# Delta net in a hybrid decoder layer: key norms and decay matrices among the convolutions, a PSUM bank of its own for the recurrence's key products, the output norm by chunks of tokens

## The chip, the cores and the metric

One core of one Trainium2 chip. The metric is the time that the device takes for one execution, in microseconds (us). Engines: TensorE (PE; PEld are its weight loads), VectorE (DVE), ScalarE (ACT), GpSimd (POOL), and SyncE (SP), which issues the DMAs. PSUM is the memory that PE's products are written to, in banks of 128 partitions by 512 float32 values; SBUF holds everything else.

## The reference

One step of one decoder layer for 1024 prompt tokens and 8 x 8 sample tokens, 1088 columns together, all in float32. Two feed-forward networks stand around a mixer; the mixer is what the change touches.

```python
x = x + 0.5 * rms_norm(swiglu_ffn(rms_norm(x, ...)), ...)       # D_MODEL 1024, D_FF 2816
qa, ka, va, qkvb, zb, ab, bb, ga, gb = split_columns(h @ w_in)  # h = rms_norm(x)
oa = swa_prompt(qa, ka, va, sinks)                              # window 128, 8 heads; swa_sample with a cache
xb = silu(causal conv of width 4 over qkvb)
qb, kb = l2_normalize(q) * 128 ** -0.5, l2_normalize(k)         # 4 heads, 128 wide
g = -exp(dn_a_log) * softplus(ab + dn_dt_bias);  beta = sigmoid(bb)
ob, s = gated_delta_chunked(qb, kb, vb, g, beta, s0)
ob = rms_norm(ob, dn_out_norm) * silu(zb)
merged = sigmoid(ga) * (oa @ w_branch_a) + sigmoid(gb) * (ob @ w_branch_b)
x = x + rms_norm(merged @ w_out);  x = x + 0.5 * (second feed-forward network)
...
# gated_delta_chunked, for each chunk of tokens: gc = cumsum(g)
decay = exp(gc_i - gc_j) for j <= i
m = strictly lower part of (beta k) @ k.T * decay;  solve (I + m) against [beta k exp(gc), beta v]
qk = (q @ k.T) * decay
def step(s, ...):
    v_new = v_u - k_cum @ s
    o = (q * exp(gc)) @ s + qk @ v_new
    s = s * g_tot + (k * exp(gc_last - gc)).T @ v_new
```

## The kernel before

**Columns and products.** Activations lie transposed: features on the partitions, the 1088 columns in three chunks (`CH`) of 384, 384 and 320. A float32 projection is made of three products of split values (high by high, high by low, low by high; lines 142 to 144). The three for one block of 128 features are called a *k-step* here; eight of them make one chunk of one *unit* of 128 output features. Projections write the banks `pa`. All other products of the mixer take banks from `pb()`, which gives `ph` and `py` in turn; `po` is one more bank, used by the attention's outputs (`po_tile()`, a single buffer).

**Order.** In the mixer PE's order is written out by hand. `queue` holds generators of projection units: `gate_unit` (ga), `z_unit` (z) and `conv_unit` (qkv: projection, convolution on DVE and ACT, SiLU; each head has one for k, q and v, in this order). `fill(us)` runs k-steps from the queue's head until their nominal times reach `us`; with an empty queue it does nothing. `finish` and `drain` run whole units. `together(a, b)` alternates between the two generators of a pair of heads: at each `yield x, y` it fills x after head a and y after head b. The other engines get their instructions in an order that a scheduler sets from the program.

**The mixer's stages**, with their approximate places in the profile: k, v, q projections to 848 us; decays of the tokens and transposes of the values (lines 773 to 810) to 854; `attention_prompt` over 16 items to 1003, whose output products, transposes and score products (L995, L979, L950) have fillers of 4.8 us between items; `attention_sample` to 1021; then for each pair of heads, 0 and 1, 2 and 3:
- their convolutions (those of head 0 serve as fillers in the attention),
- `first()`: key transposes (L1129) with copies and squares on ACT (L1130, L1131) and sums on DVE (L1132); decay matrices D and factors E from cumulated decays; the key norms, 9 columns wide (L149, L150, L1157 to L1169); q.k (L1175), D's transposes (L1177), their product on DVE (L1178), q times E on POOL (L1180); k.k (L1186) and M (L1189); value transposes (L1221),
- `invert()`: 62 DVE operations and some DMAs that invert 32x32 blocks, while PE runs `fill(51.0)`,
- `second()`: the blocks' inverse is completed; then the *recurrence*, eight steps of the state S for each head: M S (L1305) into columns 0 to 127 of a bank, U V of the next step (L1297), the key product (L1314, columns 128 to 255), the state's update on DVE (L1317), S q (L1323) and QK v (L1324) into columns 256 to 383, and a copy on ACT (L1325); then the *tail*: products with the eight sample states (L1336, 16 columns each), L1337, L1342, L1358, the sample states' update (L1366), and the output norm: sums over the head's features (L1374), the root and a Newton step over all 1088 columns, and the gate product on POOL (L1379).

After the second pair come the gate units 14 and 15 and the branch products (`br`), which need the heads' outputs, split in two (L196).

Of the kernel before, what the change touches and what calls it, by code (L numbers as in the profile page):

```python
# [7 lines left out]
F32 = mybir.dt.float32  # L8
# [27 lines left out]
def body(ctx: ExitStack, tc: tile.TileContext, d):  # L36
# [679 lines left out]

    hvd = cp.tile([P, 1], F32, tag="hvd", name="hvd")
    nc.vector.tensor_scalar_mul(hvd, vec[:, V_DN : V_DN + 1], -0.25)
    for cs in ((0, 1), (2,)):
        for u in (0, 2, 3, 4, 5, 1):  # L720
            w = wk if u == 0 and cs[0] == 0 else unit(U_K + u, f"kvq{u}_{cs[0]}")
            for c in cs:
                if u == 0:
                    do_ab(c)
                if u < 2:
                    mm = do_kv((kT, vT)[u], w, c)
                else:
                    mm = do_q(u - 2, w, c)
                if c == 1 and u in (0, 3):
                    tc.add_manual_dep(behind[u // 3].ins, mm.ins.name, NOSYNC, reason="behind products that are ready")  # L730
# [8 lines left out]
    tk = {}  # L739
    for nm, w in (("a", 36), ("x", 36), ("e", 36), ("u", 36), ("w", 36), ("z", 36), ("g", 36), ("beta", 36), ("bh", 36), ("gc", 36), ("gl", 36), ("kds", 36), ("bg", 36), ("gtot", 32), ("gts", 32), ("nea", 4)):  # L740
        tk[nm] = s2b.tile([P, w], F32, tag=f"tk_{nm}", name=f"tk_{nm}")
    def v94(t):
        return t.rearrange("p (c h) -> p c h", h=4)

    nc.vector.tensor_tensor(
        out=v94(tk["a"]), in0=atok[:, :, 0:4], in1=vec[:, V_DT : V_DT + 4].unsqueeze(1).to_broadcast([P, 9, 4]), op=ALU.add
    )
    nc.vector.tensor_scalar_mul(tk["x"], tk["a"], -1.0)
    nc.vector.tensor_tensor(out=tk["x"], in0=tk["x"], in1=tk["a"], op=ALU.min)
    nc.scalar.activation(tk["e"], tk["x"], AF.Exp)  # L750
    nc.scalar.activation(tk["nea"], vec[:, V_AL : V_AL + 4], AF.Exp)
    nc.vector.tensor_scalar_mul(tk["nea"], tk["nea"], -1.0)
    nc.vector.tensor_scalar_add(tk["u"], tk["e"], 1.0)
    nc.scalar.activation(tk["x"], tk["u"], AF.Ln)
    nc.vector.tensor_scalar_add(tk["u"], tk["u"], -1.0)
    nc.vector.tensor_scalar(out=tk["z"], in0=tk["u"], scalar1=0.0, scalar2=None, op0=ALU.is_equal)
    nc.vector.tensor_tensor(out=tk["u"], in0=tk["u"], in1=tk["z"], op=ALU.add)
    nc.vector.reciprocal(tk["w"], tk["u"])
    nc.vector.tensor_tensor(out=tk["x"], in0=tk["x"], in1=tk["w"], op=ALU.mult)
    nc.vector.tensor_tensor(out=tk["x"], in0=tk["x"], in1=tk["z"], op=ALU.add)  # L760
    nc.vector.tensor_tensor(out=tk["x"], in0=tk["x"], in1=tk["e"], op=ALU.mult)
    nc.vector.tensor_scalar_max(tk["a"], tk["a"], 0.0)
    nc.vector.tensor_tensor(out=tk["a"], in0=tk["a"], in1=tk["x"], op=ALU.add)
    nc.vector.tensor_tensor(
        out=v94(tk["g"]), in0=v94(tk["a"]), in1=tk["nea"].unsqueeze(1).to_broadcast([P, 9, 4]), op=ALU.mult
    )
    nc.vector.tensor_copy(v94(tk["beta"]), atok[:, :, 4:8])
    nc.scalar.activation(tk["beta"], tk["beta"], AF.Tanh, scale=0.5)
    nc.vector.tensor_scalar(out=tk["beta"], in0=tk["beta"], scalar1=0.5, scalar2=0.5, op0=ALU.mult, op1=ALU.add)
    nc.vector.tensor_scalar_mul(tk["bh"], tk["beta"], 0.5)  # L770
    psg = pb()
    g = tk["g"]
    nc.tensor.matmul(psg[:, 0:32], cst[:, C_TRI : C_TRI + P], g[:, 0:32], start=True, stop=True)
    nc.tensor.matmul(psg[:NSM, 32:36], cst[:NSM, C_TRIS : C_TRIS + NSM], g[:NSM, 32:36], start=True, stop=True)
    nc.tensor.matmul(psg[:, 64:96], ones, g[:, 0:32], start=True, stop=True)
    nc.tensor.matmul(psg[:NSM, 96:100], cst[:NSM, C_BONE : C_BONE + NSM], g[:NSM, 32:36], start=True, stop=True)
    for h in range(4):
        nc.tensor.matmul(
            psg[:, 128 + 8 * h : 136 + 8 * h], g[:NSM, 32 + h : 33 + h].to_broadcast([NSM, P]), cst[:NSM, C_BLK : C_BLK + 8], start=True, stop=True
        )  # L780
    for nm, o in (("gc", 0), ("gl", 64)):
        nc.vector.memset(tk[nm], 0.0)
        nc.vector.tensor_copy(tk[nm][:, 0:32], psg[:, o : o + 32])
        nc.vector.tensor_copy(tk[nm][:NSM, 32:36], psg[:NSM, o + 32 : o + 36])
    nc.scalar.activation(tk["gts"], psg[:, 128:160], AF.Exp)
    nc.vector.tensor_tensor(out=tk["kds"], in0=tk["gl"], in1=tk["gc"], op=ALU.subtract)
    nc.scalar.activation(tk["kds"], tk["kds"], AF.Exp)
    nc.scalar.activation(tk["gtot"], tk["gl"][:, 0:32], AF.Exp)
    nc.scalar.activation(tk["bg"], tk["gc"], AF.Exp)
    nc.vector.tensor_tensor(out=tk["bg"], in0=tk["bg"], in1=tk["beta"], op=ALU.mult)  # L790


    psc = pb()
    nc.tensor.transpose(psc[:36, :P], tk["gc"], ident)
    gct = s2b.tile([36, P], F32, tag="gct", name="gct")
    nc.vector.tensor_copy(gct, psc[:36, :P])
    for c in range(9):
        nc.sync.dma_start(gcd[:, c, :], gct[4 * c : 4 * c + 4, :])


    vtok = YA[6]
    vts = s2b.tile([NSM, P], F32, tag="vts", name="vts")
    for hlf in range(2):
        ps = py()
        for j in range(4):
            n = hlf * 4 + j
            nc.tensor.transpose(ps[:, j * P : (j + 1) * P], vT[:, n * P : (n + 1) * P], ident)
        nc.scalar.copy(vtok[:, hlf * 512 : hlf * 512 + 512], ps)
    ps = py()
    nc.tensor.transpose(ps[:NSM, :P], vT[:, NPR:NT], ident)  # L810
    nc.scalar.copy(vts, ps[:NSM, :P])
    for b in range(8):
        nc.sync.dma_start(d["vso"][b, 120:128, :], vts[b * 8 : b * 8 + 8, :])

# [122 lines left out]

    items = [(n, tp2) for n in range(8) for tp2 in range(2)]
# [159 lines left out]
    class Head:  # L1098
# [9 lines left out]
        def first(self):  # L1108
# [8 lines left out]
            nk = s2b.tile([P, 5, 9], F32, tag="nk", name=f"nk{h}", bufs=2)  # L1117
            ss, rho, rho2, t9, bgr = (nk[:, i, :] for i in range(5))
            nc.vector.memset(ss, 1.0)
# [4 lines left out]
            for c0 in (0, 4, 8):  # L1124
                n = 4 if c0 < 8 else 1
                w = P if c0 < 8 else NSM
                pt = pb()
                for i in range(n):
                    nc.tensor.transpose(pt[:w, i * P : i * P + P], kT_[:, (c0 + i) * P : (c0 + i) * P + w], ident)  # L1129
                nc.scalar.copy(wide(k, c0) if c0 < 8 else k8, pt[:w, : n * P])  # L1130
                nc.scalar.activation(M[:w, : n * P], pt[:w, : n * P], AF.Square)  # L1131
                nc.vector.tensor_reduce(  # L1132
                    out=ss[:w, c0 : c0 + n], in_=M[:w, : n * P].rearrange("p (i c) -> p i c", c=P), op=ALU.add, axis=AX.X
                )
# [18 lines left out]
            yield 2.0, 2.0  # L1153

            nc.scalar.activation(U, q, AF.Square, scale=P * EPS ** 0.5)
            nc.sync.dma_start(sqd[h], U)
# [12 lines left out]
            nc.vector.tensor_tensor(out=self.bhr, in0=mine("bh"), in1=rho, op=ALU.mult)  # L1169
            for j, c0 in enumerate((0, 4)):  # L1170
# [9 lines left out]
                nc.gpsimd.tensor_tensor(out=wide(q, c0), in0=wide(q, c0), in1=Es[j], op=ALU.mult)  # L1180
# [44 lines left out]
        def second(self):  # L1225
# [75 lines left out]
            for c in range(8):  # L1301
# [11 lines left out]
                yield 0.0, 0.8  # L1313
                nc.tensor.matmul(p[:, 128:256], k[:, cs], vns, start=True, stop=True)  # L1314
                S2 = ar[:, 4 + c % 2, :]
                if c > 0:
                    nc.vector.scalar_tensor_tensor(  # L1317
                        out=S2, in0=S, scalar=tk["gtot"][:, ix : ix + 1], in1=p[:, 128:256], op0=ALU.mult, op1=ALU.add
                    )
                else:  # L1320
                    nc.vector.tensor_copy(S2, p[:, 128:256])
# [5 lines left out]
                yield 0.0, 0.5  # L1327
# [12 lines left out]
            yield 0.0, 0.0  # L1340
# [21 lines left out]
            nc.scalar.activation(q, QK, AF.Square)  # L1362
            nc.vector.tensor_tensor(out=q, in0=q, in1=v, op=ALU.add)
# [8 lines left out]
            for a, b in ((0, 512), (512, 1024), (1024, NT)):  # L1372
# [269 lines left out]
```

## Time and profile before

| | us |
|---|---|
| median of 3 runs (2444.51 to 2445.79) | 2445.39 |
| the profiled execution | 2447.49 |
| its span, first instruction to last | 2445.6 |
| PE busy | 2368.5 (97%) |
| DVE busy | 1690.9 (69%) |
| ACT busy | 1091.3 (45%) |
| POOL busy | 44.2 (2%) |
| mean granted clock of PE | 0.986 |

The mixer stands between about 755 and 1490 us of the span; the feed-forward networks around it are not touched. In the rows of the profile L12 is line 12 of the kernel; a row of the waits says which engine, bank and line waited, for which engine and line, how long in all, how often, and the longest. A row of the timeline has the start, the duration, the engine, the line and the operation, the output and inputs with their shapes, and in brackets the idle time of that engine just before and what ended it. The granted clock is PE's, as a share of its full speed: at 0.5 a product takes twice as long.

### The profile page before, as it was taken

The numbers are of one execution on the slowest core, as the hardware profiler recorded it, in microseconds if no ns is written. First come the engines' busy times: TensorE is split into PE (matmuls) and PEld (weight loads), VectorE is DVE, ScalarE is ACT, GpSimd is POOL, SyncE is SP. The second block draws the span as 40 slices with busy tenths as digits, with TensorE's granted clock in tenths as the row PEclk, the third lists the DMA queues.
The fourth block names the chain that finished last, engine by engine and source line by source line (L and its number), as shares of the span: only waits on it lengthen the run. The fifth ranks groups of instructions, "written<-read, shape, count | busy, mean of one in ns | idle before, by whom it ended". The sixth has DMA issues, their size and how long they took to land. (4 is left out here: it accounts for less than half of the span.)

```text
span 2445.6 us, 38753 instructions
## 1 busy us (share of the span) xinstructions
PE 2368.5 (97%) x14535; PEld 2300.2 (94%) x14535; DVE 1690.9 (69%) x3385; ACT 1091.3 (45%) x2268; POOL 44.2 (2%) x33
## 2 busy tenths in 40 slices
PE   8999999999999999999899999999989999999997
PEld 7999999999998987999798979999989999999997
DVE  8887657757788567774497346556997576676677
ACT  7644424324475455543354333245744333233344
POOL 0000000000000000010101010000000000000000
PEclk9999999999999999999999989999999999999998
DMA  7332212213454511324222336435523122122453
GB/s 269 121 116 87 70 52 86 69 51 109 159 177 138 179 58 42 127 61 119 82 91 76 108 100 214 135 122 200 167 93 97 48 82 78 45 86 80 153 166 133
DMA packets 170373, 272.00 MB, mean 111 GB/s; under 512 B 34892, under 2 KB 74288, under 8 KB 170176
## 3 DMA queue, kind: packets, MB, share of 16 engines
q1 hardware_dynamic: 170184, 269.52, 34.2%
q8 instruction: 114, 1.87, 0.3%
q14 instruction: 75, 0.61, 0.1%
HBM read 227.03 MB, written 43.41 MB: 111 GB/s over the span
## 5 line engine op out<-in xcount | busy, mean ns | idle before, releaser
L467 PE MATMUL pa<-cl,h_c_s 128*128 128x384 f32 x704 | 236.5, 336 | 4.7 <-DVE cl L276 4.7
L466 PE MATMUL pa<-ch,h_c_s 128*128 128x384 f32 x704 | 237.6, 337 | 3.0 <-DVE t L472 2.7
L468 PE MATMUL pa<-ch,l_c_s 128*128 128x384 f32 x704 | 236.4, 336 | 0.0
L472 DVE TENSOR_TENSOR t<-pa,t 128x384 f32<-128x384 f32 x308 | 170.0, 554 | 83.1 <-PE pa L468 82.9
L466 PE MATMUL pa<-ch,h_c_a 128*128 128x384 f32 x528 | 177.1, 335 | 2.0 <-DVE t L472 1.5
L468 PE MATMUL pa<-ch,l_c_a 128*128 128x384 f32 x528 | 176.8, 335 | 0.0
L467 PE MATMUL pa<-cl,h_c_a 128*128 128x384 f32 x528 | 176.7, 335 | 0.0
L115 ACT CAST h_c_a<-r_c_a 128x512 fp32r<-128x512 f32 x132 | 81.8, 620 | 133.7 <-PE pa L467 113.5
L466 PEld LDWEIGHTS pa<-ch,h_c_s 128*128 128x128 f32 x704 | 132.9, 189 | 6.6 <-DVE t L472 6.2
L467 PEld LDWEIGHTS pa<-cl,h_c_s 128*128 128x128 f32 x704 | 133.0, 189 | 4.9 <-DVE cl L276 4.9
L468 PEld LDWEIGHTS pa<-ch,l_c_s 128*128 128x128 f32 x704 | 132.9, 189 | 0.0
L142 PE MATMUL pa<-xbh,h_ga 128*128 128x384 f32 (+1 forms) x384 | 130.7, 340 | 0.0
L115 ACT CAST h_c_s<-q_c_s 128x512 fp32r<-128x512 f32 x132 | 82.0, 621 | 104.1 <-PE pa L467 93.5
L143 PE MATMUL pa<-xbl,h_ga 128*128 128x384 f32 (+1 forms) x384 | 126.6, 330 | 0.0
L144 PE MATMUL pa<-xbh,l_ga 128*128 128x384 f32 (+1 forms) x384 | 126.6, 330 | 0.0
L466 PEld LDWEIGHTS pa<-ch,h_c_a 128*128 128x128 f32 x528 | 99.1, 188 | 2.8 <-DVE t L472 1.8
L468 PEld LDWEIGHTS pa<-ch,l_c_a 128*128 128x128 f32 x528 | 99.1, 188 | 0.0
L467 PEld LDWEIGHTS pa<-cl,h_c_a 128*128 128x128 f32 x528 | 99.1, 188 | 0.0
L142 PE MATMUL pa<-xbh,h_qkv 128*128 128x384 f32 (+1 forms) x288 | 95.6, 332 | 0.8 <-DVE t L884 0.8
L144 PE MATMUL pa<-xbh,l_qkv 128*128 128x384 f32 (+1 forms) x288 | 94.9, 330 | 0.0
L143 PE MATMUL pa<-xbl,h_qkv 128*128 128x384 f32 (+1 forms) x288 | 94.8, 329 | 0.0
L115 ACT CAST h_c_s<-r_c_s 128x512 fp32r<-128x512 f32 x44 | 27.4, 622 | 148.9 <-PE pa L467 134.7
(632 smaller groups left out, 7271.7 us busy)
## 6 DMA issues: line engine op xcount, KB each, us to landing
r_c_a<-in_up_dram SPq DMA_DIRECT2D x132, 256.0 KB
q_c_a<-in_up_dram SPq DMA_DIRECT2D x44, 256.0 KB
q_ub<-in_up_dram SPq DMA_DIRECT2D x44, 256.0 KB
r_ub<-in_up_dram SPq DMA_DIRECT2D x44, 256.0 KB
r_ua<-in_up_dram SPq DMA_DIRECT2D x42, 256.0 KB
q_ua<-in_up_dram SPq DMA_DIRECT2D x42, 256.0 KB
r_da<-in_dn_dram SPq DMA_DIRECT2D x40, 256.0 KB
q_da<-in_dn_dram SPq DMA_DIRECT2D x40, 256.0 KB
```

The lines of the kernel that those rows point to most:

```text
L115: nc.scalar.copy(hi, full)
L142: nc.tensor.matmul(ps[:, :n], hi[:, j, :], at(xh, k), start=first, stop=False)
L143: nc.tensor.matmul(ps[:, :n], hi[:, j, :], at(xl, k), start=False, stop=False)
L144: mm = nc.tensor.matmul(ps[:, :n], lo[:, j, :], at(xh, k), start=False, stop=last)
L466: nc.tensor.matmul(ps, wh[:, k, :], xh[:, k, :], start=k == 0, stop=False)
L467: nc.tensor.matmul(ps, wh[:, k, :], xl[:, k, :], start=False, stop=False)
L468: nc.tensor.matmul(ps, wl[:, k, :], xh[:, k, :], start=False, stop=k == 3)
L472: nc.vector.tensor_tensor(out=out, in0=ps, in1=other, op=ALU.add)
```

## The change

1. The tokens' decays become a function `decays()`, called among the q, k and v projections; the value transposes become `values()`, called after 4 k-steps of the first z unit.
2. `first()` is split into `decay()` (D and E), `keys()` (transposes and norms) and the rest. In pair 1, `a.keys()` and `b.keys()` follow head 1's convolutions of k and q; in pair 2 they follow those of q of the second head and v of the first. The value convolution of the second head is now directly ahead of q.k.
3. q times E goes from POOL (L1180) to DVE (L1230).
4. In the recurrence the key products of both heads go to the two halves of one `po` bank; the fillers of a step go from 0.8 + 0.5 to 0.4 us.
5. In the tail two places get fillers of 0.4 and 0.9; squares, norm and gate product go by the three chunks of columns, with the gate product on DVE (L1400) and a DMA for each chunk.
6. The attention's last item gets a filler of 8.5 us instead of 4.8, and ga4 joins the queue ahead of the sample's attention. Convolutions are run by `drain` and no longer through the queue.

```diff
+        fill(2.0)
+        values()
         attention_prompt()
-        queue += gates[3:4]
+        finish(list(queue))
+        queue += gates[3:5]
         attention_sample()
-        finish(list(queue))
-        queue += heads[1].conv
         for hs in (heads[0:2], heads[2:4]):
-            finish(list(queue))
-            queue += gates[4:10] if hs[0].h == 0 else zs[2:4] + gates[10:14]
-            together(*(x.first() for x in hs))
+            a, b = hs
+            if a.h == 0:
+                a.decay()
+                b.decay()
+                drain(b.conv[0])
+                a.keys()
+                drain(b.conv[1])
+                b.keys()
+                drain(b.conv[2])
+                queue += gates[5:10]
+            else:
+                for u in (a.conv[0], b.conv[0], a.conv[1]):
+                    drain(u)
+                a.decay()
+                b.decay()
+                drain(b.conv[1])
+                a.keys()
+                drain(a.conv[2])
+                b.keys()
+                drain(b.conv[2])
+                queue += zs[2:4] + gates[10:14]
+            together(a.first(), b.first())
             invert(hs)
...
-            fill(4.8 if 0 < it < n else 7.5)
+            fill(7.5 if it == 0 else 8.5 if it == n - 1 else 4.8)
...
-                nc.gpsimd.tensor_tensor(out=wide(q, c0), in0=wide(q, c0), in1=Es[j], op=ALU.mult)
...
+            for j, c0 in enumerate((0, 4)):
+                nc.vector.tensor_tensor(out=wide(q, c0), in0=wide(q, c0), in1=Es[j], op=ALU.mult)
...
-                yield 0.0, 0.8
-                nc.tensor.matmul(p[:, 128:256], k[:, cs], vns, start=True, stop=True)
+                yield 0.0, 0.4
+                pk = pks()[:, 128 * (h % 2) : 128 * (h % 2) + 128]
+                nc.tensor.matmul(pk, k[:, cs], vns, start=True, stop=True)
...
-                yield 0.0, 0.5
+                yield 0.0, 0.0
...
-            for a, b in ((0, 512), (512, 1024), (1024, NT)):
+            for a, b in CH:
+                cs = slice(a, b)
                 pq = pb()
-                nc.tensor.matmul(pq[:, : b - a], ones, q[:, a:b], start=True, stop=True)
-                nc.scalar.activation(k[:, a:b], pq[:, : b - a], AF.Identity, scale=1.0 / P, bias=eps4)
-            nc.scalar.activation(v, k, AF.Abs_reciprocal_sqrt)
-            newton(v, k, M)
-            nc.vector.scalar_tensor_tensor(out=QK, in0=QK, scalar=hvd, in1=v, op0=ALU.mult, op1=ALU.mult)
-            nc.gpsimd.tensor_tensor(out=QK, in0=QK, in1=U, op=ALU.mult)
-            nc.sync.dma_start(obd[h], QK)
+                nc.tensor.matmul(pq[:, : b - a], ones, q[:, cs], start=True, stop=True)
...
+                nc.vector.tensor_tensor(out=QK[:, cs], in0=QK[:, cs], in1=U[:, cs], op=ALU.mult)
+                nc.sync.dma_start(obd[h, :, cs], QK[:, cs])
```

PE's order in the recurrence of the first pair, from its first key product on. Before (`ph` and `py` are the two heads' banks; `pa` is a filler's):

```order
L1314 MATMUL ph_12336<-s_8355,s_8352 128x128
L1324 MATMUL ph_12336<-s_8354,s_8355 128x128
L1314 MATMUL py_12339<-s_8347,s_8340 128x128
L1324 MATMUL py_12339<-s_8346,s_8347 128x128
L142 MATMUL pa_12298<-xbh_1_8284,h_ga_1_12096 128x320
L143 MATMUL pa_12298<-xbl_1_8286,h_ga_1_12096 128x320
L144 MATMUL pa_12298<-xbh_1_8284,l_ga_1_12097 128x320
```

After, L1333 being the key product, L1343 the old L1324, L1323 the old L1305, and L1315 the old L1297:

```order
L1333 MATMUL po_12367<-s_8355,s_8352 128x128
L1343 MATMUL ph_12351<-s_8354,s_8355 128x128
L1333 MATMUL po_12367<-s_8347,s_8340 128x128
L1343 MATMUL py_12354<-s_8346,s_8347 128x128
L1323 MATMUL ph_12360<-s_8355,s_8351 128x128
L1323 MATMUL py_12362<-s_8347,s_8345 128x128
L1315 MATMUL ph_12382<-s_8350,s_8353 128x128
L1315 MATMUL py_12384<-s_8344,s_8341 128x128
```

Both heads' key products now write one `po` bank, and the step's end has no filler.

DVE's order at the end of the second head's value convolution in pair 1, after the change (L865 to L893 are the convolution, L1195 the product of q.k with D, L1230 that of q with E):

```order
L885 TENSOR_SCALAR t_963_11495<-t_962_11491,vec 128x64
L887 TENSOR_SCALAR t_964_11500<-t_962_11491,vec 128x64
L889 COPY sn_11503<-ncv 128x3
L890 COPY sn_11503<-t_962_11491 128x24
L888 TENSOR_TENSOR t_963_11495<-t_963_11495,t_964_11500 128x64
L1195 TENSOR_TENSOR s_8354<-ph_11520,s_8355 128x512
L887 TENSOR_SCALAR t_964_11500<-t_962_11491,vec 128x64
L1195 TENSOR_TENSOR s_8346<-ph_11534,s_8347 128x512
L888 TENSOR_TENSOR t_963_11495<-t_963_11495,t_964_11500 128x64
L1230 TENSOR_TENSOR s_8348<-s_8348,s_8355 128x512
```

Before, the sums and norms of the keys stood between the convolution and this product (L1178 then), with POOL doing q times E:

```order
L1132 TENSOR_REDUCE nk_11363<-s_8351 64x1
L1157 TENSOR_SCALAR nk_11363<-nk_11363 128x9
L1132 TENSOR_REDUCE nk_11432<-s_8345 64x1
L1178 TENSOR_TENSOR s_8354<-ph_11494,s_8355 128x512
L1157 TENSOR_SCALAR nk_11432<-nk_11432 128x9
L1178 TENSOR_TENSOR s_8346<-ph_11519,s_8347 128x512
L149 TENSOR_TENSOR nk_11363<-nk_11363 128x9
```

The norms are now ahead of this place, and the convolution's rest and the q-by-E products stand beside L1195.

More of the change, by code (lines that the diff above doesn't have):

```diff
@@ L728, in body @@
                     mm = do_q(u - 2, w, c)
+                if c == 2 and u == 4:
+                    decays()
                 if c == 1 and u in (0, 3):
@@ L757, in body @@
[L757 to L780, printed above, removed]
@@ L936, in gate_unit, with values @@
             yield from gate_do(i, w, c)
+    def values():
+        for hlf in range(2):
+            ps = py()
+            for j in range(4):
+                n = hlf * 4 + j
+                nc.tensor.transpose(ps[:, j * P : (j + 1) * P], vT[:, n * P : (n + 1) * P], ident)
+            nc.scalar.copy(vtok[:, hlf * 512 : hlf * 512 + 512], ps)
+        ps = py()
+        nc.tensor.transpose(ps[:NSM, :P], vT[:, NPR:NT], ident)
+        nc.scalar.copy(vts, ps[:NSM, :P])
+        for b in range(8):
+            nc.sync.dma_start(d["vso"][b, 120:128, :], vts[b * 8 : b * 8 + 8, :])
     items = [(n, tp2) for n in range(8) for tp2 in range(2)]
@@ L1106, in __init__, with decay @@
             self.conv = [conv_unit(u * 4 + h, A[u]) for u in (1, 0, 2)]
-        def first(self):
+        def decay(self):
             h = self.h
@@ L1122, in first @@
             DS, eR, DT = d8[:w8, 0, :], d8[:, 1, :], d8[:w8, 2, :]
[L1124 to L1134, printed above, removed]
             for j, c0 in enumerate((0, 4)):
@@ L1152, in first, with keys @@
             nc.scalar.activation(eR, QK[:, cs8], AF.Exp)
-            yield 2.0, 2.0
-            nc.scalar.activation(U, q, AF.Square, scale=P * EPS ** 0.5)
-            nc.sync.dma_start(sqd[h], U)
+            self.D = Ds, Es, DS, eR, DT
+        def keys(self):
+            h = self.h
+            q, kT_, v, M, k, U, QK, R = self.A
+            k8 = self.k8
+            nk = s2b.tile([P, 5, 9], F32, tag="nk", name=f"nk{h}", bufs=2)
+            ss, rho, rho2, t9, bgr = (nk[:, i, :] for i in range(5))
+            nc.vector.memset(ss, 1.0)
+            for c0 in (0, 4, 8):
+                n = 4 if c0 < 8 else 1
+                w = P if c0 < 8 else NSM
+                pt = pb()
+                for i in range(n):
+                    nc.tensor.transpose(pt[:w, i * P : i * P + P], kT_[:, (c0 + i) * P : (c0 + i) * P + w], ident)
+                nc.scalar.copy(wide(k, c0) if c0 < 8 else k8, pt[:w, : n * P])
+                nc.scalar.activation(M[:w, : n * P], pt[:w, : n * P], AF.Square)
+                nc.vector.tensor_reduce(
+                    out=ss[:w, c0 : c0 + n], in_=M[:w, : n * P].rearrange("p (i c) -> p i c", c=P), op=ALU.add, axis=AX.X
+                )
             nc.vector.tensor_scalar_add(ss, ss, 4.0 * EPS)
@@ L1223, in first, with second @@
             yield 0.0, 0.0
-        def second(self):
+        def second(self, pks):
             h = self.h
```

143 lines of the change are left out of this document (86 added, 57 removed).

## The prediction

> **What bounds the kernel now.** I read the page's totals and clock first, then the waits of TensorE (PE) between 750 and 1500 us, the mixer, the one stage whose code the change touches; then windows around them for the granted clock; then the timeline at the places that the change edits.
>
> ```profile
> span 2445.6 us, 38753 instructions
> PE 2368.5 (97%) x14535; PEld 2300.2 (94%) x14535; DVE 1690.9 (69%) x3385; ACT 1091.3 (45%) x2268; POOL 44.2 (2%) x33
> ```
>
> PE is the bound over the whole span: 2445.6 - 2368.5 = 77 us are idle. No matmul is removed, so the change can only take back idle time and time at half clock. The next two views say how much of either lies in the mixer: first the waits (PE bank, line <- what released it: us in total, times, longest), then windows (length, busy time of PE, PEld, DVE, ACT, POOL, granted clock, DMA).
>
> ```profile
> PE ph L1323 <- DVE s L1317: 6.5, 14, 0.6
> PE py L1323 <- DVE s L1317: 6.2, 14, 0.4
> PE ph L1186 <- DVE s L1178: 4.2, 2, 2.2
> PE ph L979 <- DVE s L833: 3.5, 1, 3.5
> PE pa L142 <- DVE t L1470: 2.5, 1, 2.5
> PE ph L1129 <- ACT s L1131: 2.3, 1, 2.3
> PE pa L142 <- DVE t L672: 2.1, 2, 1.4
> ```
> ```profile
> 850.00:858.00 8.00, 6.95 (x29) 6.02 (x29) 3.41 (x14) 3.50 (x15) 0.00 (x0) 0.57 0.14 41
> 977.00:981.00 4.00, 3.27 (x14) 3.30 (x15) 3.97 (x9) 1.77 (x5) 0.00 (x0) 0.57 0.06 12
> 1021.00:1025.00 4.00, 4.00 (x17) 3.96 (x16) 2.71 (x10) 2.51 (x5) 0.00 (x0) 0.57 0.39 108
> 1058.00:1073.00 15.00, 12.20 (x94) 11.68 (x92) 14.68 (x45) 9.80 (x24) 5.12 (x4) 1.00 0.15 50
> 1153.00:1194.00 41.00, 33.89 (x230) 30.77 (x231) 12.01 (x35) 11.79 (x39) 0.00 (x0) 1.00 0.18 58
> 1286.00:1304.00 18.00, 13.43 (x81) 12.63 (x79) 15.83 (x40) 11.07 (x27) 5.42 (x5) 0.81 0.20 66
> 1304.00:1309.00 5.00, 4.38 (x23) 4.03 (x24) 3.83 (x18) 1.17 (x2) 0.00 (x0) 0.66 0.01 2
> 1427.00:1449.00 22.00, 21.99 (x75) 14.15 (x74) 10.28 (x17) 6.47 (x13) 3.79 (x2) 0.61 0.43 132
> 1475.00:1490.00 15.00, 10.41 (x49) 9.48 (x48) 13.61 (x30) 10.43 (x24) 0.00 (x0) 0.89 0.94 293
> ```
>
> The seven waits add up to 27 us. A stretch at clock c for L us loses (1 - c) x L: 3.4, 1.7, 1.7, 3.4 (1286:1304), 1.7 (1304:1309), 8.6 and 1.7 us, 22 us in all. So some 50 us can be had in the stage; the sum below asks how much of it the edits reach.
>
> **E, the recurrence (two pairs of heads).** One step in the timeline of PE (start, duration), and the update of the state on VectorE (DVE):
>
> ```profile
> 1168.58 0.38 PE L1305 MATMUL ph<-s,s 128*128 128x128 f32 x2
> 1169.65 0.34 PE L143 MATMUL pa<-xbl,h_ga 128*128 128x384 f32 x1
> 1170.17 0.34 PE L143 MATMUL pa<-xbl,h_ga 128*128 128x384 f32 x1
> 1170.52 0.38 PE L1314 MATMUL ph<-s,s 128*128 128x128 f32 x2
> 1171.34 0.49 PE L1323 MATMUL ph<-s,s 128*128 128x128 f32 x2 [0.44 <-DVE s L1317]
> 1171.89 0.39 PE L1314 MATMUL py<-s,s 128*128 128x128 f32 x2
> 1172.72 0.49 PE L1323 MATMUL py<-s,s 128*128 128x128 f32 x2 [0.44 <-DVE s L1317]
> 1173.79 0.38 PE L1305 MATMUL ph<-s,s 128*128 128x128 f32 x2
> ```
> ```profile
> 1170.94 0.35 DVE L1317 SCALAR_TENSOR_TENSOR s<-s,tk_gtot,ph 128x128 f32<-128x128 f32 x1 [1.32 <-PE ph L1314]
> ```
>
> A step lasts 1173.79 - 1168.58 = 5.21 us: ten 128x128 products at 0.22 (1171.89 less 1171.34 is 0.55 for two, with a 0.1 restart), three filler k-steps at 0.52 (1170.17 - 1169.65), and twice 0.6 in which PE stands between L1314 and L1323 (0.82 apart instead of 0.22). The cause: L1314 and L1323 write the same bank, and DVE reads that bank in L1317, which starts 0.42 after L1314 and takes 0.35. After the change the key product goes to a bank of its own, so the query product of the same head no longer waits. But both heads share that bank: head b's product waits until head a's update has left it. By hand, from the start of head a's product: a's query product follows at 0.22, its last product at 0.44, and head b's key product could start at 0.66; the update is done at 0.42 + 0.35, and PE goes on 0.06 later, at 0.83. So it waits 0.17 once a step in place of 1.22. Head a's next use of the state comes far behind 0.83. The filler drops from three k-steps to one; the others are only run elsewhere. A step is then 10 x 0.22 + 0.52 + 0.17 = 2.9 us. Gain per pair 8 x 1.05 = 8.4, both 17. DVE and ScalarE (ACT) also evacuate filler, at half a microsecond each, and may stand ahead of an update: 12 is the lower bound; the whole of the stall, 8 x 1.22 x 2 = 19.5, the upper. I take 17, nearer to the top since the filler's share falls.
>
> **F, the tail behind each recurrence** (products with the sample states, norm sums).
>
> ```profile
> 1194.38 1.85 PE L1336 MATMUL ph<-mq,s 128*128 128x16 f32 x16
> 1212.46 0.42 PE L142 MATMUL pa<-xbh,h_qkv 128*128 128x384 f32 x1
> 1427.51 1.85 PE L1336 MATMUL ph<-mq,s 128*128 128x16 f32 x16
> 1449.18 1.02 PE L1374 MATMUL ph<-s,eye 128*128 128x512 f32 x2
> ```
>
> The first tail takes 18.1 us, the second about 23 (to the end of that row and a 64-column rest). The second lost 8.6 to the clock: the work is 14.4, so the excess is 8.6 + 3.7 = 12.3. In both the queue of fillers had run dry before the last waits. Since the recurrence will use 16 k-steps less per pair, the tail finds 1 + 2 + 4 + 10 of them, at the places where PE otherwise issues 16-column products that leave the clock low. I take -8.5; -4 if 16-column products halve the clock even with k-steps between; -11 if nearly all goes.
>
> **G, the branch products after the gates** wait 2.5 (L1470) and 2.1 (L672) and lose 1.7 to the clock: 6.3. They wait for splits of the heads' output on DVE, which come behind the last norm. Now the norm goes out in three chunks, with the gate product on DVE instead of the slower POOL, and 12 k-steps of ga13 (6.2 us) stand before these products. -4, from 0 (DVE is the limit here: 13.61 of 15 busy) to -6.3.
>
> **A, decays and value transposes** leave the empty place before the attention's first item and go among the k/v/q projections and behind 4 k-steps of z0. Window 850:858 shows PE idle for 1.05 and 3.4 lost: -3.5, from -2 to -4.5. **B, the attention's last items**: fill 8.5 instead of 4.8 at the last. The 3.5 wait (L979 for the softmax, with DVE busy 3.97 of 4 behind convolution work) comes before that fill, and moves only because the work before it shifts by some 4 k-steps; with the half clock behind it 5.2 are at stake. I take half, -2.5 (0 to -5.2). **C**, the half clock at 1021 (1.7): the sample's empty fill now finds ga4: -1 (0 to -1.7).
>
> **D, convolutions and first() of both pairs.** The old first(): PE, then DVE, then POOL.
>
> ```profile
> 1058.36 0.60 PE L1129 MATMUL ph<-eye,s 128*128 128x128 f32 x4
> 1065.46 1.05 PE L1175 MATMUL ph<-s,s 128*128 128x128 f32 x8
> 1070.34 0.60 PE L1177 MATMUL py<-eye,R 128*128 128x128 f32 x4
> 1073.15 1.16 PE L1186 MATMUL ph<-s 128*128 128x128 f32 x8 [2.21 <-DVE s L1178]
> ```
> ```profile
> 1058.56 0.42 DVE L672 SCALAR_TENSOR_TENSOR t<-pa,r 128x256 f32<-128x256 f32 x1
> 1063.31 0.22 DVE L897 TENSOR_TENSOR t<-t,t 128x64 f32<-128x64 f32 x1
> 1066.55 0.69 DVE L1178 TENSOR_TENSOR s<-ph,s 128x512 f32<-128x512 f32 x1
> 1069.26 1.34 DVE L150 SCALAR_TENSOR_TENSOR nk<-nk 128x9 f32<-128x9 f32 x2
> ```
> ```profile
> 1066.60 2.60 POOL L1180 TENSOR_TENSOR s<-s,s 128x512 f32<-128x512 f32 x2 [10.13 <-PE ph L1175]
> ```
>
> Now the key transposes, norms and decays stand among the convolutions, and q.k comes directly behind the value convolution. Removed: the two 9-column norm operations of 0.67 each while POOL's L1180 runs, and the 2.2 wait behind them. Added: q.k of head a's second half needs the bank that DVE frees in L1195 (old L1178), and in DVE's order L1195 stands behind the value convolution's rest: 1058.56 to 1063.31 is 4.8, less a reduction of 0.6, plus two 0.6 steps that moved in: L1195 ends about 6.2 us after the last convolution matmul. PE reaches that product after half of what q.k and the decay transposes take in all (1070.34 - 1065.46 + 0.43 = 5.3), 2.66: wait 3.6. The rest is DVE-paced: four L1195 and four of POOL's products, now on DVE, at 0.6 each, so that k.k starts 9.2 after the last convolution instead of 14.8 - 4.2 (fill) - 2.2 (transposes) = 8.4: +0.8. About +1 for the transposes' own waits among the convolutions, where ACT also changes tables. With a half clock behind the 3.6 (1.7): +3.5 in pair 1, whose old first() ran at clock 1.00. In pair 2 the old one had 4.6 idle, and 3.4 + 1.7 lost, so the same new state gives -2. Together +1.5; from -6 (DVE keeps up, no half clock) to +9 (DVE paces the convolutions too).
>
> Whether that half clock comes is the open point. In the rows, a wait of 2.2 within 1058:1073 left the clock at 1.00, while in pair 2 a wait of 2.0 ahead of 1304 was followed by 0.66.
> [...]
>
> **Sum:** E -17, F -8.5, G -4, A -3.5, B -2.5, C -1, D +1.5 = -35. The profiled span of 2445.6 becomes 2410.6. The profiled execution took 2447.5, 1.9 more, and the median of the runs is 2445.4, 2.1 below that: so 2410 for the median.
>
> **Rivals.**
> 1. *The shared bank becomes the new chain.* If filler evacuation on DVE stands ahead of the update in most steps, head b's product waits 0.9 (0.17 + 0.35 + 0.4) instead of 0.17: 16 x 0.73 = 12 back, 2422. For it: the bank serves both heads. Against: DVE is busy 12.01 of 41 in 1153:1194, and less filler runs than before.
> 2. *DVE paces convolutions and first().* D at +9: 2418. For it: DVE 15.83 of 18 and 14.68 of 15 in the old stages, and POOL's products added. Against: what blocked DVE behind POOL goes away.
> 3. *Nearly all idle goes*: A -4.5, B -5.2, C -1.7, D -6, E -19.5, F -11, G -6.3: 2391.
> 4. *Slower: the recurrence falls to half clock.* With one k-step instead of three it is nearly all 128x128 products; if these don't hold the clock, each step's 2.72 us doubles: 16 x 2.72 = +43, 2453. It decides from 13 of the 16 steps on (35 / 2.72). Against: 1153:1194 ran at 1.00 with 7.1 us of 41 idle, and 1065.46 to 1070.34, only such products, at 1.00 too.
>
> **Numbers.** The forecast (2402 to 2416) 0.50; rival 1 alone 0.12; rival 2 alone 0.16, both together 0.05 (2430); rival 3 0.11; rival 4 0.03; no change for a reason not seen 0.03. The range 2395 to 2428 leaves out the last two, the two rivals together, and most of rival 3. A difference of 0.2%, 5 us, is about what a measurement of this kernel tells from none: faster 0.94, same 0.03, slower 0.03.
>
> **What would show it.** After: the wait for the state's update at the query product gone, a wait of 0.2 to 0.3 at the second head's key product, a step of 2.9 us; clock near 1 in the second tail; a new wait of 3 to 5 us at q.k in each first(); the 2.5 at L1470 gone. The forecast is wrong if the recurrence step is over 3.5 us, or if the convolutions show waits for DVE in the projections' banks.

## The result, and the profile after

Median 2416.75 us (4 runs, 2412.53 to 2420.05) against 2444.95 (4 runs, 2438.46 to 2445.79): ratio 0.9889, 95% interval 0.9864 to 0.9915, so 28 us faster. Timed again beside the last experiment the same kernel gave 2416.79 and 0.989 (0.987 to 0.9911). The profiled execution took 2414.26 us and lies 2.5 us below the median of its runs, as that of before (2447.49) lies 2.5 above its own; its span, on which the accounts below are made, is 33 us shorter than that of before. 30 us of these lie in the mixer: from the same product ahead of it to the same product behind it, 761.7 us became 731.7. The other 3 lie in the second feed-forward network, which is not changed and whose length differs by as much from run to run (below).

The totals of the page after:

```profile
span 2412.4 us, 38783 instructions
PE 2354.2 (98%) x14535; PEld 2295.1 (95%) x14535; DVE 1688.5 (70%) x3437; ACT 1103.4 (46%) x2300; POOL 22.1 (1%) x21
```

PE's idle time went from 77 to 58 us, and its busy time fell by 14 with the same instructions. Some 8.5 us of the 14 are the clock: in the mixer 47.8 us ran at half clock before and 30.7 after, and half of such a stretch is lost (after, the 128x384 products at 971.5 to 972.1, at half clock, start 0.31 to 0.33 us apart, those from 972.9 on, at full clock, 0.17). The waits of PE in the mixer after:

```profile
PE ph L1192 <- DVE s L1195: 8.6, 2, 4.9
PE ph L983 <- DVE t L888: 3.1, 1, 3.1
PE ph L1255 <- DMA s<-ud: 2.1, 1, 2.1
PE pa L142 <- DVE t L1518: 1.0, 1, 1.0
PE po L1333 <- DVE s L1340: 0.5, 2, 0.3
```

The 12.7 us of waits in the recurrences are gone. The largest wait is now the one at q.k (L1192), which did not exist before. Windows after:

```profile
850.00:858.00 8.00, 7.76 (x51) 7.25 (x50) 3.55 (x9) 2.71 (x8) 0.00 (x0) 1.00 0.46 144
1020.00:1030.00 10.00, 10.00 (x76) 8.90 (x75) 2.98 (x12) 3.50 (x8) 0.00 (x0) 1.00 0.25 72
1062.00:1082.00 20.00, 15.80 (x109) 14.62 (x108) 17.96 (x53) 6.96 (x16) 0.95 (x1) 0.83 0.14 36
1156.00:1179.00 23.00, 22.66 (x171) 21.05 (x169) 11.49 (x34) 10.53 (x37) 0.00 (x0) 1.00 0.22 71
1274.00:1296.00 22.00, 16.46 (x118) 15.05 (x118) 19.27 (x64) 10.20 (x22) 2.33 (x1) 0.84 0.23 56
1393.00:1422.00 29.00, 28.50 (x130) 23.63 (x129) 11.96 (x26) 9.45 (x21) 3.79 (x2) 0.82 0.37 112
```

The decays' old place (850:858) and the sample's end (1020:1030) run at full clock (the latter not in every profile, see below); the recurrence (1156:1179) is almost without a gap; first() of either pair (1062:1082, 1274:1296) loses some 4 to 5.5 us idle and 3.5 to the clock; the second tail still loses 29 x 0.18 = 5.2 to the clock. One step of the recurrence after, on PE:

```profile
1163.85 0.39 PE L1323 MATMUL ph<-s,s 128*128 128x128 f32 x2
...
1165.31 0.38 PE L1333 MATMUL po<-s,s 128*128 128x128 f32 x2
1165.53 0.39 PE L1342 MATMUL ph<-s,s 128*128 128x128 f32 x2
1165.75 0.39 PE L1343 MATMUL ph<-s,s 128*128 128x128 f32 x2
1166.13 0.49 PE L1333 MATMUL po<-s,s 128*128 128x128 f32 x2
...
1166.90 0.39 PE L1323 MATMUL ph<-s,s 128*128 128x128 f32 x2
```

The query product (L1342) follows its key product at 0.22, as forecast, and head b's key product (1166.13) comes 0.38 after L1343 instead of 0.22: the forecast wait of 0.17 is 0.16. A step lasts 3.05 us, where the forecast had 2.9.

For each stage, its time less that of its products at the pace of undisturbed ones of the same shape, before and after in the two profiles:

| term | lost before | lost after | change | forecast |
|---|---|---|---|---|
| A projections and decays | 10.6 | 7.9 | -2.7 | -3.5 |
| B prompt attention | 37.5 | 37.8 | +0.3 | -2.5 |
| C sample attention | 3.7 | 1.7 | -2.0 | -1 |
| D convolutions and first(), pair 1 | 5.9 | 8.9 | +3.0 | +3.5 |
| D the same, pair 2 | 13.6 | 9.8 | -3.8 | -2 |
| inversion and start of second() | 2.8 | 5.0 | +2.2 | 0 |
| E recurrences | 23.5 | 6.1 | -17.4 | -17 |
| F tails | 13.0 | 8.6 | -4.4 | -8.5 |
| G branch products | 7.2 | 1.6 | -5.6 | -4 |
| sum | 117.8 | 87.4 | -30.4 | -35 |

### The profile page after: what moved, and what is told of

It is laid out like the page before. It is cut to its first block, busy times and chain, and to the rows that moved or that the text cites. A ratio compares the mean times of both kernels' runs of the same rounds, so it can differ in the third digit from the quotient of the medians.

```text
span 2412.4 us, 38783 instructions
## 1 busy us (share of the span) xinstructions
PE 2354.2 (98%) x14535; PEld 2295.1 (95%) x14535; DVE 1688.5 (70%) x3437; ACT 1103.4 (46%) x2300; POOL 22.1 (1%) x21
## 4 chain that ended last, share of the span: by engine, by line
PE 81%; DVE 9%; DMA 4%; ACT 3%; issue 2%; SPq 0%; DVEq 0%; ACTq 0%
PE pa L142 10%; PE pa L143 10%; PE pa L144 10%; PE pa L466 8%; PE pa L467 8%; PE pa L468 8%; PE py L349 3%; PE py L348 3%; PE ph L348 3%; PE ph L349 3%; PE ph L347 3%; PE py L347 3%; DVE t L865 1%; DMA q_da<-in_dn_dram 1%; DMA q_db<-in_dn_dram 1%
## 5 line engine op out<-in xcount | busy, mean ns | idle before, releaser
L144 PE MATMUL pa<-xbh,l_qkv 128*128 128x384 f32 (+1 forms) x288 | 94.1, 327 | 0.0
L143 PE MATMUL pa<-xbl,h_qkv 128*128 128x384 f32 (+1 forms) x288 | 94.1, 327 | 0.0
```

The source lines that it names most:

```text
L143: nc.tensor.matmul(ps[:, :n], hi[:, j, :], at(xl, k), start=False, stop=False)
L144: mm = nc.tensor.matmul(ps[:, :n], lo[:, j, :], at(xh, k), start=False, stop=last)
```

## Experiments

Each is the changed kernel with one edit; the last, best, joins three. Times are spans of one profiled execution beside 2412.4, and lengths of the mixer beside 731.7. Ten executions of the changed kernel had spans from 2410.6 to 2418.1, so a difference of a few us between two spans decides nothing; the mixer (731.6 in a second profile of the changed kernel), the waits and the lengths of the stages are read instead, and differences of under 1 us are not.

One thing blurs these too. In the mixer of the profiles before and after the granted clock is either full or half, and it was half for 3.41 us at a time (969.2 to 972.6 in the profile after), or for 6.83, 10.24 (after) and 17.07 (before), at 1.7 us lost for each 3.41. Where such a stretch falls moves with small shifts in time. At the sample's end, where the profiles of the changed kernel have none, the clock in 1018:1032 is 0.76 to 0.88 in e1, e3, e8, e9 and best, whose edits do not touch that place.

**Bank or fillers? e1.** The key product goes back into the step's own bank, with the fillers as changed.

```diff
-                pk = pks()[:, 128 * (h % 2) : 128 * (h % 2) + 128]
+                pk = p[:, 128:256]
```

> The changed kernel with the key product back in columns 128 to 255 of the step's own bank, fillers still 0.4. Theory 'bank' (the waits came from the query product writing the bank that the state's update reads): two waits of 0.6 us or more come back in each step, each recurrence grows by 8 to 12 us from 22.3, and the span goes from 2412 to 2428 to 2436. Rival 'fillers' (ACT and DVE were held up by the evacuation of the fillers, of which there are now a third): the recurrence stays within 3 us of 22.3, span 2412 to 2416.

Span 2437.7. The recurrences last 31.4 and 31.1 us instead of 22.6 and 22.2. Waits and one step on PE:

```profile
PE py L1342 <- DVE s L1336: 6.2, 14, 0.4
PE ph L1342 <- DVE s L1336: 6.1, 14, 0.4
```
```profile
1169.78 0.39 PE L1323 MATMUL ph<-s,s 128*128 128x128 f32 x2
...
1171.20 0.38 PE L1333 MATMUL ph<-s,s 128*128 128x128 f32 x2
1172.02 0.49 PE L1342 MATMUL ph<-s,s 128*128 128x128 f32 x2 [0.44 <-DVE s L1336]
...
1173.94 0.39 PE L1323 MATMUL ph<-s,s 128*128 128x128 f32 x2
```

The old 0.82 between key and query product is back, 28 waits of it, and the step is 4.16, 1.1 more. That is the forecast's 1.05. The span is 1.7 us over the bound given for the theory: the recurrences make 17.6 of the mixer's 21.5, the rest is in the tails (3.5) and small parts.

**e2** puts the fillers back (0.8 and 0.5 in place of 0.4 and 0).

> The changed kernel with the recurrence's fillers back at 0.8 and 0.5 us. Theory 'bank': a step is 2.9 plus two k-steps of 0.52, about 3.9 to 4.0, with no wait over 0.3 at the key or query products; the 32 k-steps are missing in the tails, so the span is 2414 to 2420. Rival 'fillers': waits of 0.4 to 0.6 come back at the query products, step 4.8 or more, span over 2424.

Span 2416.0; recurrences 31.1 and 30.2 us, that is 8.5 and 8.0 more for 16 k-steps of 0.52, with no wait at the query products:

```profile
PE pa L142 <- DVE t L1518: 3.1, 2, 2.0
PE po L1333 <- DVE s L1336: 1.0, 1, 1.0
PE po L1333 <- DVE s L1340: 0.7, 2, 0.5
```

So the bank alone ended the waits. Fewer fillers are a matter of where the k-steps go: the mixer is 5.5 longer. At its end the branch products (first row) wait 3.1 instead of 1.0. The larger loss is in the first tail, which now has no k-step instead of 17 and stands at half clock for 17.1 us (8.5 lost, beside 1.7 in the changed kernel):

```profile
1185.00:1208.00 23.00, 22.09 (x72) 13.76 (x73) 10.27 (x23) 7.50 (x17) 3.79 (x2) 0.63 0.39 119
```

**e3** issues both key products next to each other, by a `yield 0.0, 0.0` behind the key product.

> The changed kernel with both heads' key products issued next to each other, ahead of both updates. If head b's product waited for head a's update in each step (0.17 by the prediction's hand count, 16 times), the recurrences shrink from 22.6 and 22.2 us by 1 to 1.5 each, span 2409 to 2411. If the count was wrong and nothing waits there in most steps, they stay within 0.4 and the span within 1 us of 2412.

Span 2409.2; recurrences 20.9 and 20.3, 1.7 and 2.0 shorter, and the wait of L1333 is gone from the list. The prediction's wait at the shared bank was there in every step: 0.16 in all steps but three, longer (0.5 and 0.3) in the first step of each pair and shorter (0.1) in one last step. That makes 1.6 and 1.4 us; what the other 0.1 and 0.6 are was not traced.

**Was it worth it to spread the key norms? e7** puts all convolutions first, then both `keys()`.

> The changed kernel with all convolutions first, then both heads' key transposes and norms, then the rest of first(). Theory 'DVE order' (q.k's bank is freed late because the value convolution's rest stands ahead on DVE): the key part moves the same wait to the key transposes and norms, so from the last convolution to the first k.k it takes about 14 us instead of 11.9 in pair 1 and 14 in place of 12.5 in pair 2, in sum 2 to 6 us more, span 2414 to 2420. Rival (putting the norms among the convolutions brought nothing, DVE's total decides): span within 2 us of 2412.

Span 2412.1, mixer 730.0: no loss, as the rival had it. From q.k to k.k it takes 8.0 and 7.5 us instead of 11.9 and 12.5, and what the key transposes wait cancels it: from the sample attention or the first tail to the end of the value transposes it takes 58.0 and 94.1 us, beside 58.2 and 93.9. The waits:

```profile
PE ph L1192 <- ACT s L1159: 3.1, 2, 1.6
PE ph L1157 <- ACT s L1159: 2.7, 2, 1.8
PE py L1157 <- ACT s L1159: 1.9, 2, 0.9
```

7.7 in sum in place of 8.6 at L1192, and the wait for the inversion's DMA is not in this profile. The part of the change that its name puts first brought nothing measurable. What PE waits for differs, though: DVE with the rest of the value convolution in the changed kernel, ACT with the copies and squares of the key transposes (L1158, L1159) here. So it is not DVE's total that decides, as the rival's wording says, but two engines in turn at about the same price.

**e5** fills that wait: `fill(4.8)` ahead of `together(a.first(), b.first())`.

> The changed kernel with a 4.8 us filler (10 k-steps) between the last convolution and first() in both pairs. Theory 'DVE order': PE only waited for DVE to finish the value convolution's rest; the waits of 3.8 and 4.9 at q.k fall below 1 in sum, the half clock behind them (6.8 in the profile, four windows) goes, span 2398 to 2404. Rival 'DVE total': the fillers' own evacuations delay DVE as much, waits of 5 us or more remain, or the time comes back where the 20 k-steps now lack (tails, branch products): span 2408 to 2413.

Span 2408.0, mixer 724.8: 7 us shorter. The same stretches, from the filler to k.k:

```profile
1061.00:1077.00 16.00, 16.00 (x129) 15.45 (x128) 15.51 (x46) 6.94 (x14) 0.00 (x0) 1.00 0.23 66
1268.00:1287.00 19.00, 19.00 (x147) 18.49 (x146) 18.72 (x62) 10.70 (x21) 0.00 (x0) 1.00 0.21 63
```

PE is busy all of the time, at full clock; DVE nearly so. The 8.6 us of waits and 6.8 of lost clock (6.83 us at half clock in each pair) are gone, and q.k to k.k takes 5.4 and 5.3. Of these 15.4 us more than half came back: the branch products wait 3.2 in sum instead of 1.0 and then stand at half clock for 3.41 us, and the first tail, with 8 k-steps instead of 17, loses 5 us to the clock instead of 1.7. The span is the rival's lower bound; the mechanism is the theory's, the return the rival's second half.

**e8** takes the output norm whole again, with the gate product on POOL.

> The changed kernel with squares, norm and gate product over all 1088 columns again, the gate product on POOL. Theory 'chunks' (the branch products no longer wait since the last norm goes out by chunks): waits of 3 to 5 us come back ahead of the branch products, span 2415 to 2420. Rival 'cover' (12 k-steps of ga13 in front of the branch products did it): these waits stay within 1.5 us, span 2412 to 2415.

Span 2415.6, mixer 737.5, 5.7 longer. Its waits:

```profile
PE ph L1192 <- DVE s L1195: 12.0, 2, 8.2
PE pa L142 <- DVE t L1516: 2.2, 1, 2.2
```

At the branch products the wait is 1.2 longer, between the two expectations, and a half clock of 3.41 us follows that the changed kernel does not have (1.7 lost). More of the loss is in pair 2: from the first tail to its value transposes it takes 3.7 us longer, and its q.k waits 8.2 instead of 4.9. The norm of pair 1 lies on DVE at the start of pair 2's convolutions in either kernel; new is that POOL's two gate products each hold up an operation of DVE with two inputs:

```profile
1208.76 3.48 POOL L1398 TENSOR_TENSOR s<-s,s 128x1088 f32<-128x1088 f32 x1 [24.29 <-DVE s L1397]
1215.78 2.87 POOL L1398 TENSOR_TENSOR s<-s,s 128x1088 f32<-128x1088 f32 x1 [3.54 <-DVE s L1397]
```
```profile
1209.74 2.90 DVE L865 SCALAR_TENSOR_TENSOR t<-t,vec,t 128x384 f32<-128x384 f32 x1
1216.50 2.69 DVE L116 TENSOR_TENSOR l_qkv<-r_qkv,h_qkv 128x512 fp32r<-128x512 f32 x1
```

Neighbouring operations of the same lines take 0.61 and 0.68, so the two stand for some 4.3 us. The edit changes the chunks and the engine together; what the chunks alone are worth was not run.

**e9** gives q times E back to POOL (L1230, `nc.gpsimd` instead of `nc.vector`).

> The changed kernel with q times E on POOL again, at the place in the program where the change has it. The prediction held that POOL's operations block DVE's two-input ones: then the eight products of some 1.3 us keep DVE, which at that place has the matrices M to compute, back by 1 to 5 us per pair, the inversion starts later, and the wait for its DMAs grows from 2.1 us to 4 or more: span 2414 to 2420. Rival: DVE is relieved by eight operations of 0.6 per pair and nothing waits for POOL: span 2408 to 2412.

Span 2423.7, mixer 736.4. The waits at q.k are 12.1 in sum instead of 8.6. POOL, then DVE, in pair 2:

```profile
1280.96 2.81 POOL L1230 TENSOR_TENSOR s<-s,s 128x512 f32<-128x512 f32 x2 [13.26 <-PE ph L1192]
```
```profile
1280.86 0.16 DVE L861 COPY ncv<-t 128x3 f32<-128x3 f32 x1
1281.17 1.48 DVE L893 SCALAR_TENSOR_TENSOR s<-t,t 128x384 f32<-128x384 f32 x1 [0.15 <-ACT t L892]
1282.58 1.22 DVE L889 COPY sn<-ncv 128x3 f32<-128x3 f32 x1
```

While POOL works from 1280.96 to 1283.77, an operation of DVE with two inputs from SBUF (L893) takes 1.48 us and a copy of three columns behind it 1.22; the copy ahead takes 0.16. In the changed kernel the same lines take at most 0.57 and 0.18. Giving eight operations of 0.69 us to POOL made DVE later, not earlier. The place differs from the expected one (q.k, not the inversion), and only 4.7 of the span's 11 us lie in the mixer; 5.0 lie behind it and 1.7 ahead of it, where the edit changes nothing. The copy behind L893 has one input, and it ends with POOL's second product. In the profile of before a copy of three columns took 2.52 us beside the gate product on POOL, up to its end:

```profile
1218.92 3.48 POOL L1379 TENSOR_TENSOR s<-s,s 128x1088 f32<-128x1088 f32 x1 [18.46 <-DVE s L1378]
```
```profile
1219.90 2.52 DVE L870 COPY ncv<-t 128x3 f32<-128x3 f32 x1
```

The other copies of that line take at most 0.17. So an operation with one input was held up as well; why, no run shows.

**e6** puts one k-step behind the third and one behind the sixth of the eight 16-column products of a head (`if b in (3, 6): fill(0.4)`).

> The changed kernel with one k-step after the third and one after the sixth of the eight 16-column products with the sample states, per head. Theory: those products hold the clock at a half though PE counts as busy; with k-steps among them the half clock of the tails (1.7 and 5.1 us lost) goes, tails plus convolutions up to 5 us shorter, span 2407 to 2409. Rival: their pace or waits set the tail; clock unchanged, span 2411 to 2413.

Span 2411.0, mixer 729.7. Both tails:

```profile
1178.00:1201.00 23.00, 22.74 (x125) 18.35 (x124) 10.52 (x23) 8.63 (x19) 3.79 (x2) 1.00 0.49 148
1393.00:1419.00 26.00, 25.24 (x138) 20.46 (x138) 13.71 (x25) 9.00 (x19) 3.79 (x2) 1.00 0.41 124
```

The clock is 1.00 in both (0.93 and 0.82 before the edit), and they are 1.6 and 2.8 us shorter, the second with 21 k-steps instead of 18. Since such stretches move, one profile is not enough, but the other profiles say the same. Without this edit (before, the changed kernel twice, and the nine other experiments) the clock fell to half during or directly behind the 16-column products in 22 of 24 tails; with it (e6 and best) in none of four. So the half clock goes with the 16-column products, while PE counts as busy (in the changed kernel 23.74 of 24 us in 1178:1202 at 0.93, 28.50 of 29 in 1393:1422 at 0.82). The two exceptions, the first tail of e3 and the second in the second profile of the changed kernel, show that they do not always. The branch products then wait 3.0 instead of 1.0, and of the gain 2 us are left.

**The wait in the attention: e4** moves the 8.5 us filler one item ahead (`n - 2`); **e10** puts head 0's convolutions ahead of the gates in the queue.

> The changed kernel with the attention's 8.5 us filler one item earlier. Theory: the wait of 3.1 at the transposes (for the softmax, with convolution work ahead of it on DVE) stands in front of the filler, not behind it; with the filler moved it goes down to under 0.5, and so does the half clock behind it (1.7): span 2407 to 2409. Rival: the filler's own convolution work delays the softmax by as much again, or the next item waits instead: wait over 2 us in sum, span 2411 to 2413.

> The changed kernel with head 0's convolutions ahead of the first three gate units in the queue, so that the last attention items have gates as fillers. Theory: the 3.1 us wait at the transposes comes from convolution operations in DVE's and ACT's queues ahead of the softmax; it goes to an earlier item or vanishes, and none stays at the last items. If it vanishes with its half clock the span is 2406 to 2409; if waits like it turn up among the earlier items, 2411 to 2416. Rival: it belongs to the last items themselves (their order) and stays at 3.

e4: span 2417.0, mixer 733.2. The wait did not move, and a new one of 0.9 came behind it:

```profile
PE ph L983 <- DVE t L888: 3.1, 1, 3.1
PE ph L983 <- DVE s L824: 1.5, 2, 0.9
```
```profile
969.54 0.67 PE L983 MATMUL ph<-eye,s 128*128 128x128 f32 x4 [3.14 <-DVE t L888]
...
980.67 0.48 PE L954 MATMUL ph<-s,s 64*128 64x256 f32 x1
```

But this edit does not try the theory. Within an item the filler comes after the transposes, so at `n - 2` the 8.5 us run directly behind the transposes that wait (17 k-steps between these two rows), and at `n - 1` one item later still. To stand ahead of them the filler would have to be at `n - 3`; that was not run.

e10: span 2417.1, mixer 736.0:

```profile
PE ph L983 <- DVE s L824: 8.5, 5, 4.3
```

With the convolutions as early fillers five items wait, 8.5 us in all, the longest at 940.5, and the last ones no longer do. So the wait goes with the convolutions' work on DVE ahead of the softmax, and not with the last items. Whether a longer filler ahead of the waiting transposes would cover it stays open.

**The edits together: best** has e3, e6, and e5 with 4.4 us.

> The changed kernel with three of the edits together: both key products first, 4.4 us of filler ahead of first(), k-steps among the 16-column products. If their gains in the mixer add up (3.5, 7.0 and 2.0 by the profiles), less 2 because the branch products now find fewer k-steps ahead of them, the span is 2400 to 2404 and the ratio to the kernel before 0.983. If the fillers are missing more than that, 2405 to 2409.

> The changed kernel as it is, for the comparison on the same chip: 2412 to 2420, ratio 0.987 to 0.991. Its runs differ by some 7 us; if that comes from the second feed-forward network (as the two profiles, 3 us apart there, say) the mixer's part is within 1.5 us of 731.7.

Median 2400.87 (5 runs, 2396.38 to 2405.31), ratio to the kernel before 0.9826 (0.9804 to 0.9848), beside 0.989 (0.987 to 0.9911) of the changed kernel in the same comparison: the intervals do not meet. The profile's span is 2403.4 and the mixer 719.8, 11.8 shorter than that of the changed kernel. Its first tail has one half clock of 6.8 us, which follows three short waits of PE (0.3 to 0.5) at the products that update the sample states, and not the 16-column products. What is left in it:

```profile
PE pa L142 <- DVE t L1522: 3.2, 2, 2.2
PE ph L983 <- DVE t L888: 3.1, 1, 3.1
PE ph L1255 <- DMA s<-ud: 1.0, 1, 1.0
```

The branch products, the attention's softmax and the inversion. The lengths behind the mixer were 919.2 to 925.5 us over these profiles, for the same instructions; what sets them was not tried, nor what makes the runs of one kernel differ by 7 us (the second profile of the changed kernel was again one of 2414 us, so it does not tell).

## Why the prediction was right, and where it was not

The forecast was 2410 (2395 to 2428); the median is 2416.8, the change 28 us instead of 35. The time lies just above the narrower forecast (2402 to 2416) and next to rival 2's 2418, but that is chance: rival 2's term, D, came out at -0.8 and not at +9. Rivals 1, 3 and 4 fell as well: no filler stood ahead of the updates, F and B gave less and not more, and the clock in 1156:1179 is 1.00.

- **E, half of the gain, was right** in mechanism (e1, e2) and size (-17.4 for -17). The shared bank's wait of 0.17 was measured as 0.16, and e3 took it away.
- **D was right in what it named, and near in sum** (-0.8 for +1.5). PE waits at q.k (forecast 3.6; measured 3.8 and 4.9), and a half clock of 6.83 us sets in within the wait in both pairs (at 1068.2 and 1279.8), 3.4 lost each time. That it would come, and cost 1.7, was the author's estimate; no run shows that such a wait always costs as much. From q.k to k.k pair 1 took 11.9 us with two stretches of half clock, and 10.7 with one in the second profile; the forecast was 9.2 and one stretch of 1.7. So after the same wait of 3.8 us the clock cost 3.4 or 1.7, and the open question, when a wait is followed by half clock, is not settled by the length of the wait. Two pieces were off: the 1 us for the transposes' own waits has no row after, and pair 2's -2 sets only the old lost clock against the new state (3.5 - 5.1); with its old idle time too, 4.6 against 2.8 in pair 1, the same sum gives -3.4, and -3.8 was measured. In the working of the 3.6, the terms named (4.8 - 0.6 + 1.2) make 5.4 and not 6.2; the difference is about L1195's own 0.7, which is not named. The prediction did not ask whether the spread of the norms was worth anything; e7 says that it was not.
- **F was mis-sized**: -4.4 for -8.5. The failed step is that k-steps between the groups would keep the clock up. They help (e2, without any in the first tail, loses 8.5 us there to the clock), but they stand behind sixteen records of 16 columns, too late; e6 shows what it takes. The lower bound (-4) had named just this case.
- **B failed**: the half of 5.2 us that a shift by some k-steps was to bring did not come (+0.3 in the whole prompt attention; the wait is 3.1 where it was 3.5). The prediction had said that the filler of 8.5 stands behind this wait. e10 shows that the wait goes with the convolutions.
- **C gave -2.0 for -1, of which 1.7 is luck**: the half clock that is gone there is back in five of the later profiles.
- **G came out a little better** (-5.6 for -4). Of the reasons given, chunks and the faster engine (1.6 us on DVE for a head's gate product, 3.48 and 2.87 on POOL in e8) carry about 2.6 at that place (e8: 1.2 of wait, the rest clock); taking k-steps away from it costs 2 to 4 (e2, e5, e6).
- **Not in the sum**: the inversion. The prediction let k.k and M come later and did not count that the inversion starts from M; its DMAs now end 2.1 us after PE's fillers in pair 2. Where k.k comes earlier this wait is shorter or gone (0.7 in e5, none in e7).
- The rest is which executions were profiled: the profile of before stands 2.5 us above its median and that of after 2.5 below, so the profiles show 33 us where the medians show 28.

## What to carry to other kernels

When PE waits between two products of one step, look whether they write the bank that another engine is to read between them; a bank of its own, even one shared by two heads, ended 12.7 us of waits, and issuing both writers first ended the rest. With PE at 97% a moved piece of work is only worth the idle time, or the time at half clock, at its new place: here the queue of fillers is fixed, so each k-step put into one gap left another open in the tails or at the branch products. Ask of every relief of DVE through POOL what DVE runs at that moment (in e9 L893 took 1.48 us beside POOL instead of at most 0.57). And before an experiment that moves a filler, read in the order of PE on which side of the wait it will stand.

## What the runs showed of the hardware

The granted clock fell to half behind 16-column products that kept PE busy by the record (tail windows at 0.93 and 0.82), in 22 of 24 tails over twelve profiles, and in none of four with two k-steps among a head's sixteen records (e6, best). In the recurrence, ten 128-column products to one k-step held it at 1.00 (1156:1179 after). PE's share of busy time did not tell the two apart: 22.66 of 23 us in that stretch of the recurrence, 28.50 of 29 in the tail at 0.82. Operations of DVE took longer beside POOL's products: with two inputs, 1.48 us instead of at most 0.57 (e9), 2.90 and 2.69 instead of 0.61 and 0.68 (e8); with one, copies of three columns, 1.22 instead of at most 0.18 (e9) and 2.52 instead of at most 0.17 (before).
